# Two FFN and mixing layers in split fp32 on one core: earlier start of the next sublayer, another order of an attention pair, and a final update spread over three engines

## The chip, the cores and the metric

The kernel runs on one core of a Trainium2 chip. The metric is device time in microseconds (us) of one execution. The engines of the core are TensorE (PE; its weight loads are listed as PEld), VectorE (DVE), ScalarE (ACT), GpSimd (POOL) and SyncE (SP), whose queue issues the DMAs. Each engine works through its own instructions in the order in which the program emits them; semaphores hold an instruction until what it reads or overwrites is ready.

## The reference

Two layers work on 384 tokens of width 1024 in fp32: 128 prompt tokens and 256 latent tokens. Each layer has three sublayers: an FFN, a mixing sublayer and a second FFN. Cut to what matters here:

```
for l in range(2):
    h = modulate(x, npre[0], shift, scale)                  # rmsnorm * gain * (1 + scale) + shift
    x = x + 0.5 * gate * rmsnorm(swiglu(h, fw_in[0], fw_out[0]), npost[0])
    h = modulate(x, npre[1], ...)
    q, k, v, f, g = split(h @ w_in)                         # 512, 512, 512, 256, 512 columns
    o = concat(attn(q, k, v), fourier_mix(f), gmlp_mix(g))  # 8 heads of 64; rpb is a bias per head
    x = x + gate * rmsnorm(o @ w_out, npost[1])
    h = modulate(x, npre[2], ...)
    x = x + 0.5 * gate * rmsnorm(swiglu(h, fw_in[1], fw_out[1]), npost[2])
```

The attention of the latent tokens adds `rpb`, a table of biases for each head, to the scores, and also attends to 128 cached keys and values. The prompt tokens attend among themselves. The Fourier part transforms 256 channels, and the gated part passes 512 columns through gelu.

## The kernel before

Activations lie transposed, channels on partitions and tokens along the free axis, so that one tile is 128 channels by 384 tokens. Every weight product is done as three matmuls of a reduced fp32 type. A weight tile (`raw`, 128x1024) is split into `whi`, a cast on ACT (L160), and `wlo`, a subtraction on DVE (L170); `mm3` then multiplies hi by hi, hi by lo and lo by hi, eight times for a tile of eight k blocks. The weights of the whole program form one stream. Three raw tiles and six split tiles are held; the load of raw tile i+3 is put on SP's queue right after the subtraction that frees the buffer of raw tile i, and waits there for that subtraction. What the program puts on SP's queue later stands behind it. `take` hands the next split tile to the products and lets the stream split one tile more (`split_ahead`).

A sublayer ends in a `Post` object. `Post.add(m)` takes output tile m: a square on ACT (L483), its addition to `accy` on POOL (L485, for all but the first and the last tile), and a scaled copy `yg`. `all` sums the squares over partitions with matmuls against a matrix of ones (L206), `std` takes the root on ACT (L501). The next sublayer's `Enter` object is made by the function `after`, which computes the gain A on DVE (L227) and calls `begin`: five ACT instructions and three DVE instructions on tile 0 of x and of yg (L268 to L273). In an FFN `after` runs behind the products of output tile 6 of 0 to 7; in the mixing sublayer inside tile 7, behind its first two k blocks and behind the addition of tile 6. The next sublayer's `group` then runs its first five or six products before the norm of its input is known, carries two columns more per tile for the shift (386 columns), and multiplies by the reciprocal root afterwards (`biased`). From tile `switch` on, an FFN uses normed inputs (384 columns).

The mixing sublayer starts with `leave`: DVE scales a finished product tile into `t` (L460) and ACT applies gelu, or nothing for the Fourier and attention tiles, and writes it in two pieces (L716). Tiles 0 and 1 (`g0`, `g1`) and 2 and 3 (`ut`) are gelu tiles, tile 4 (`t0`) is a Fourier tile. `turn` transposes a tile on PE (L740) into one of two PSUM banks `px`; ACT copies it out (L787, L788 into `gv`). `channels` is the Fourier product over channels (L749) and uses a `px` bank too.

Attention goes in four pairs of heads. The order of a pair is a string, `PAIR` for the first three and `LAST` for the fourth. U is the value product of the pair before; A0 and A1 the scores; S0 and S1 the softmax steps on DVE and ACT (L830 adds the bias and takes the maximum, L833 and L839 are the exponentials, L842 to L845 the division), each for both heads of the pair (e0, e1); F00, F10, F01 and F11 the transposes of the probabilities (`flip`, L854 on PE, copied out by L858 and L860 on ACT), the first digit being the head; K0, K1, Q0, Q1, W0 and W1 are halves of the next pair's key, query and value products; L scales the next value tile, t transposes it (copied out by L914), k, c and q finish keys, cached keys and queries. The second half of K, Q and W also lets the stream split a tile. b issues the four DMAs of the next pair's `rpb` tables on SP (L683), and two additions on POOL for each head build `biases` from them (L689), which S0 of the next pair reads.

At the very end `finish` updates x for the last time: a reciprocal of the root on DVE (L509), then a multiplication (L514) and an addition (L515) for each pair of tiles, the 128 prompt tokens on POOL and the 256 latent tokens on DVE, and a DMA of each result (L516).

## Time and profile before

| | |
|---|---|
| median of 3 runs | 1476.79 us (1475.21 to 1476.86) |
| profiled execution, its own time | 1476.81 us |
| its span in the trace | 1475.0 us, so 1.8 us lie around the span |
| granted TensorE clock, mean | 0.991 |
| busy: PE, DVE, ACT, POOL | 98%, 78%, 47%, 14% |
| chain that ended last, by engine | PE 87%, DVE 5%, ACT 4% |

The busy shares say how much of the span an engine worked. The chain is followed back from the last instruction to what released each step. A PE at 98% leaves little idle time in all, so single places where PE waits are what the other views have to show: the list of PE's waits, and the timelines around them. In a timeline row the first number is the start in us from the beginning of the span, the second the time that the row covers, then engine, line, operation and tiles, the number of instructions that were drawn together, and in brackets the idle time before the row and what ended it.

### The profile page before, as it was taken

How to read it: one execution, taken by the hardware profiler on the slowest of the kernel's cores; microseconds unless marked ns; L12 is line 12 of the kernel's file. 1: busy time of each engine (PE TensorE's matmuls, PEld its weight loads, DVE VectorE, ACT ScalarE, POOL GpSimd, SP SyncE). 2: the span in 40 equal slices, each digit the busy share in tenths (PEclk: the TensorE clock that was granted, in tenths of full speed). 3: DMA queues.
4: the chain of work that ended last, by engine and by line, in shares of the span. 5: the costliest groups of instructions: out<-in, count | busy, mean ns of one | idle time of the engine just before them, and what ended most of it. 6: DMA issues, size and time to landing. Idle time of an engine off the chain costs nothing.

```text
span 1475.0 us, 22364 instructions
## 1 busy us (share of the span) xinstructions
PE 1443.1 (98%) x8459; PEld 1410.3 (96%) x8459; DVE 1151.2 (78%) x1859; ACT 688.3 (47%) x1262; POOL 207.7 (14%) x172
## 2 busy tenths in 40 slices
PE   9999999999999999999999999999999999999996
PEld 7999999999899999999999999999989999999995
DVE  3789999987768999969989998677877699755333
ACT  3663334346656753333257333433666657333330
POOL 1100000122214130001130300010323321100012
PEclk8999999999999999999999999999999999999998
DMA  9457777845533347757824577576254324554431
GB/s 377 157 175 238 242 243 240 262 151 148 130 83 100 120 152 248 240 175 252 260 83 158 190 241 220 166 220 199 85 144 110 122 63 152 173 172 134 118 104 43
DMA packets 87004, 254.04 MB, mean 172 GB/s; under 512 B 21872, under 2 KB 26224, under 8 KB 85872
## 3 DMA queue, kind: packets, MB, share of 16 engines
q1 hardware_dynamic: 86896, 252.62, 54.2%
q8 instruction: 66, 1.08, 0.3%
q14 instruction: 42, 0.34, 0.1%
HBM read 249.96 MB, written 2.62 MB: 171 GB/s over the span
## 4 chain that ended last, share of the span: by engine, by line
PE 87%; DVE 5%; ACT 4%; issue 2%; DMA 2%; SPq 0%; POOL 0%; DVEq 0%; ACTq 0%; POOLq 0%
PE ps L187 26%; PE ps L188 26%; PE ps L189 26%; DVE wlo L170 2%; ACT whi L160 1%; PE ps L416 1%; PE ps L417 1%; PE ps L419 1%; DMA x<-in_x_dram 1%; PE ps L206 1%; PE ps L870 1%; DMA raw<-in_ffn_w_in_dram 1%; PE ps L854 1%; PE ps L815 1%; DVE t L460 0%
## 5 line engine op out<-in xcount | busy, mean ns | idle before, releaser
L170 DVE TENSOR_TENSOR wlo<-raw,whi 128x1024 fp32r<-128x1024 f32 (+1 forms) x318 | 402.1, 1269 | 189.1 <-ACT whi L160 187.7
L160 ACT CAST whi<-raw 128x1024 fp32r<-128x1024 f32 x324 | 330.9, 1027 | 395.9 <-PE ps L188 364.1
L102 DVE CUSTOM_DVE_ANT_0 junk<-adaw,cb,adab 128x1024 bf16<-128x1024 f32 x256 | 334.5, 1307 | 11.2 <-DMA adaw<-in_ada_w_dram 6.6
L188 PE MATMUL ps<-nlo,whi 128*128 128x384 f32 x896 | 299.3, 334 | 0.0
L187 PE MATMUL ps<-nhi,whi 128*128 128x384 f32 x896 | 299.3, 334 | 0.0
L189 PE MATMUL ps<-nhi,wlo 128*128 128x384 f32 x896 | 299.3, 334 | 0.0
L187 PE MATMUL ps<-hhi,whi 128*128 128x386 f32 (+1 forms) x789 | 276.2, 350 | 0.0
L188 PE MATMUL ps<-hlo,whi 128*128 128x386 f32 (+1 forms) x789 | 269.0, 341 | 1.8 <-DVE hlo L244 1.7
L189 PE MATMUL ps<-hhi,wlo 128*128 128x386 f32 (+1 forms) x789 | 268.8, 341 | 0.7 <-DVE wlo L170 0.7
L187 PE MATMUL ps<-ahi,whi 128*128 128x384 f32 x768 | 257.2, 335 | 0.0
L188 PE MATMUL ps<-alo,whi 128*128 128x384 f32 x768 | 256.7, 334 | 0.0
L189 PE MATMUL ps<-ahi,wlo 128*128 128x384 f32 x768 | 256.6, 334 | 0.0
L485 POOL TENSOR_TENSOR accy<-accy,sqy 128x384 f32<-128x384 f32 x36 | 53.7, 1491 | 818.6 <-ACT sqy L483 818.4
L187 PEld LDWEIGHTS ps<-nhi,whi 128*128 128x128 f32 x896 | 168.2, 188 | 0.0
L188 PEld LDWEIGHTS ps<-nlo,whi 128*128 128x128 f32 x896 | 168.2, 188 | 0.0
L189 PEld LDWEIGHTS ps<-nhi,wlo 128*128 128x128 f32 x896 | 168.2, 188 | 0.0
L187 PEld LDWEIGHTS ps<-hhi,whi 128*128 128x128 f32 x789 | 149.9, 190 | 5.3 <-issue 3.1
L188 PEld LDWEIGHTS ps<-hlo,whi 128*128 128x128 f32 x789 | 149.9, 190 | 5.1 <-DVE hlo L244 3.6
L189 PEld LDWEIGHTS ps<-hhi,wlo 128*128 128x128 f32 x789 | 149.7, 190 | 1.3 <-DVE wlo L170 1.3
L187 PEld LDWEIGHTS ps<-ahi,whi 128*128 128x128 f32 x768 | 144.2, 188 | 0.3 <-DVE hlo L136 0.3
L188 PEld LDWEIGHTS ps<-alo,whi 128*128 128x128 f32 x768 | 144.2, 188 | 0.0
L189 PEld LDWEIGHTS ps<-ahi,wlo 128*128 128x128 f32 x768 | 144.2, 188 | 0.0
(177 smaller groups left out, 1412.6 us busy)
## 6 DMA issues: line engine op xcount, KB each, us to landing
raw<-in_ffn_w_in_dram SPq DMA_DIRECT2D x176, 512.0 KB, 4.1
adaw<-in_ada_w_dram SPq DMA_DIRECT2D x128, 512.0 KB, 4.2
raw<-in_ffn_w_out_dram SPq DMA_DIRECT2D x64, 512.0 KB, 4.2
raw<-in_w_in_dram SPq DMA_DIRECT2D x36, 512.0 KB, 4.3
raw<-in_ffn_w_out_dram SPq DMA_DIRECT2D x32, 384.0 KB, 3.7
piece<-in_ada_first_dram SPq DMA_DIRECT2D x8, 1024.0 KB, 9.2
raw<-in_w_out_dram SPq DMA_DIRECT2D x16, 512.0 KB, 3.6
rpb<-in_rpb_dram SPq DMA_DIRECT2D x32, 96.0 KB, 6.4
```

Source lines behind the costliest of these rows:

```text
L102: nc.vector.tensor_tensor_reduce(out=junk, in0=w, in1=cb[:, j, :], scale=1.0, scalar=adab[:, l, b, f:f + 1], op0=ALU.mult, op1=ALU.add, ac ...
L160: nc.scalar.copy(highs[i][:, :w], raws[i][:, :w])
L170: (eng or nc.vector).tensor_tensor(out=lo[:, :w], in0=raws[i][:, :w], in1=hi[:, :w], op=ALU.subtract)
L187: nc.tensor.matmul(ps, whi, hhi, start=start, stop=False)
L188: nc.tensor.matmul(ps, whi, hlo, start=False, stop=False)
L189: nc.tensor.matmul(ps, wlo, hhi, start=False, stop=stop)
L206: nc.tensor.matmul(ps, ones, sq, start=start, stop=stop)
L416: nc.tensor.matmul(ps[g][:, :n], w[g][0][:, ks], hhi, start=False, stop=False)
L417: nc.tensor.matmul(ps[g][:, :n], w[g][1][:, ks], hhi, start=False, stop=False)
L419: nc.tensor.matmul(ps[g][:, :n], w[g][0][:, ks], hlo, start=False, stop=False)
L485: nc.gpsimd.tensor_tensor(out=self.acc, in0=self.acc, in1=sq, op=ALU.add)
L815: nc.tensor.matmul(ps[e][:, :T], q[r, qs], k[r, :], start=i == 0, stop=i == 2)
```

## The change

Five places are changed.

1. In the FFN and in the mixing sublayer `after` runs ahead of the take and the products of output tile 6. In the mixing sublayer it so stands ahead of the splits of two weight tiles and of the additions of tiles 5 and 6 in each engine's order.
2. At the start of the mixing sublayer the Fourier tile `t0` leaves first, and the stream splits one tile between the `v` and the `ut` tiles.
3. In `PAIR` the flips of the first key tile stand behind the halves of the query product, and t, b and k behind Q1.
4. `switch` is rounded down where it was rounded up: FFNs with five first products use the normed input from tile 14 on in place of 16. The first FFN has six and is not touched.
5. `finish` is written anew: the sums of squares are taken with tokens on partitions, the root and reciprocal work on three columns, and matmuls spread the result over the partitions into a PSUM bank. DVE multiplies tile by tile; the addition is done on POOL (tiles 0, 2, 4, 6), on PE with a copy out by ACT (tiles 1, 3, 5) or on DVE (tile 7), and each tile has its DMA.

```diff
@@ -37,7 +37,7 @@
 GROUP = 5
 LEAD = 3
 FIRST = 6
-PAIR = "U A0 K0 S0 A1 K1 L F00 S1 Q0 F10 t b k Q1 c n F01 F11 q W0 d W1"
+PAIR = "U A0 K0 S0 A1 K1 L Q0 F00 S1 F10 Q1 t b k c n F01 F11 q W0 d W1"
 LOADS = "S1 w0 S0 x0 k0 w1 x3 w2 S2 x1 S3 x2 w3 S4 S5 S6 x4 S7 x5 w4 c1 c0 x6 w5 x7"
@@ -501,19 +501,43 @@
             nc.scalar.activation(self.sy, self.ps, AF.Sqrt, scale=1.0 / D, bias=eps[:, 0:1])
         def finish(self):
-            self.all()
-            self.std()
-
-            r, yg = self.sy, self.yg
-            for _, b, e in RANGES:
-                nc.vector.reciprocal(r[:, b:e], r[:, b:e])
-            for m in range(0, KT, 2):
-                for (_, b, e), eng in zip(RANGES, (nc.gpsimd, nc.vector)):
-                    new, old = yg[:, m:m + 2, b:e], x[:, m:m + 2, b:e]
-                    rb = r[:, b:e].unsqueeze(1).to_broadcast([P, 2, e - b])
-                    eng.tensor_tensor(out=new, in0=new, in1=rb, op=ALU.mult)
-                    eng.tensor_tensor(out=new, in0=new, in1=old, op=ALU.add)
-                    nc.sync.dma_start(out=o["y"][:, m:m + 2, b:e], in_=new)
+
+            yg, c = self.yg, 3
+            sums = [bank(px)[:, :2 * c].rearrange("p (t j) -> p t j", j=2) for _ in range(2)]
+            for ps, sq in zip(sums, (self.acc, self.sq)):
+                for t in range(c):
+                    nc.tensor.matmul(ps[:, t, :], sq[:, t * P:t * P + P], ones[:, :2], start=True, stop=True)
+                if sq is self.acc:
+                    early = small("sy")[:, :c]
+                    nc.scalar.activation(early, ps[:, :, 0], AF.Identity, scale=1.0 / D, bias=eps[:, 0:1])
+            held = {}
+
+            def hold(m):
+                held[m] = bank()[:, :T]
+                nc.tensor.matmul(held[m], ident, x[:, m, :], start=True, stop=False)
+
+            hold(1)
+            r = small("r")[:, :c]
+            nc.vector.scalar_tensor_tensor(out=r, in0=sums[1][:, :, 0], scalar=1.0 / D, in1=early, op0=ALU.mult, op1=ALU.add)
+            nc.scalar.activation(r, r, AF.Sqrt)
+            nc.vector.reciprocal(r, r)
+            out = act.tile([P, KT, T], F32, tag="nlo", name="out")
+            rb = bank()[:, :T]
+            for t in range(c):
+                nc.tensor.matmul(rb[:, t * P:t * P + P], r[:, t:t + 1].to_broadcast([P, P]), ident, start=True, stop=True)
+            hold(3)
+            for m in range(KT):
+                new = yg[:, m, :]
+                nc.vector.tensor_tensor(out=new, in0=new, in1=rb, op=ALU.mult)
+                if m == 1:
+                    hold(5)
+                if m in held:
+                    nc.tensor.matmul(held[m], ident, new, start=False, stop=True)
+                    new = out[:, m, :]
+                    nc.scalar.copy(new, held[m])
+                else:
+                    (nc.vector if m == KT - 1 else nc.gpsimd).tensor_tensor(out=new, in0=new, in1=x[:, m, :], op=ALU.add)
+                nc.sync.dma_start(out=o["y"][:, m, :], in_=new)
     def spread(n, i, of):
         return n * (i + 1) // of - n * i // of
@@ -525,7 +549,7 @@
             ahi = fp.tile([P, FT, T], F32R, name="ahi")
             alo = fp.tile([P, FT, T], F32R, name="alo")
-            switch = len(ps) + KT + 2 + len(ps) % 2
+            switch = len(ps) + KT + 2 - len(ps) % 2
             base = at[0]
             def leave(m):
@@ -628,6 +652,8 @@
             post = Post(l, s)
             last = None
             for m in range(KT):
+                if m == KT - 2:
+                    after(post)
                 p = bank()[:, :T]
                 for c, (b, e) in enumerate(((0, 8), (8, 16), (16, 22))):
                     w, = take()
@@ -637,8 +663,6 @@
                     if m < KT - 1:
                         ada_some(spread(ada_out, m * 3 + c, 3 * KT - 3))
                 last = p
-                if m == KT - 2:
-                    after(post)
             post.add(KT - 1, last)
         return post
@@ -776,13 +800,13 @@
+            t0 = leave(ps[4], v[:, 2, :T], SAME)
             g0 = leave(ps[0], v[:, 0, :T], GELU)
             g1 = leave(ps[1], v[:, 1, :T], GELU)
+            split_to(at[0] + 3)
             leave(ps[2], ut[:, 0, :], GELU)
             leave(ps[3], ut[:, 1, :], GELU)
-            pf0 = ps[4]
             split_to(at[0] + HOLD - 1)
-            t0 = leave(pf0, v[:, 2, :T], SAME)
             pf1 = project(False)
             nc.scalar.copy(gv[:, :, 0:P], turn(g0))
             nc.scalar.copy(gv[:, :, P:], turn(g1))
@@ -967,13 +991,13 @@
                 products(p, w3[i], oparts, [7])
             enter.restore()
             for m in range(3, KT):
+                if m == KT - 2:
+                    after(post, following)
                 w, = take()
                 p = bank()[:, :T]
                 products(p, w, oparts, range(2))
                 for i in range(3) if m == 3 else [m - 1]:
                     post.add(i, outs[i])
-                if m == KT - 1:
-                    after(post, following)
                 products(p, w, oparts, range(2, KT - 1))
                 products(p, w, oparts, [KT - 1])
                 outs.append(p)
```

Three places of the order that the changed program gives its engines follow; line numbers grow by 24 in this part of the file. First ACT at the start of layer 0's mixing sublayer, before, from the table load for gelu to t0's two pieces (v takes g0, g1 and t0, one after the other in pieces of 128 and 256 columns):

```order
L716 ACT_TABLE_LOAD
L716 ACTIVATE v<-t,b 128x128
L716 ACTIVATE v<-t,b 128x256
L716 ACTIVATE v<-t,b 128x128
L716 ACTIVATE v<-t,b 128x256
L716 ACTIVATE ut<-t,b 128x128
L716 ACTIVATE ut<-t,b 128x256
L716 ACTIVATE ut<-t,b 128x128
L716 ACTIVATE ut<-t,b 128x256
L160 CAST whi<-raw 128x1024 x3
L716 ACTIVATE v<-t,b 128x128
L716 ACTIVATE v<-t,b 128x256
```

and now:

```order
L740 ACTIVATE v<-t,b 128x128
L740 ACTIVATE v<-t,b 128x256
L740 ACT_TABLE_LOAD
L740 ACTIVATE v<-t,b 128x128
L740 ACTIVATE v<-t,b 128x256
L740 ACTIVATE v<-t,b 128x128
L740 ACTIVATE v<-t,b 128x256
L160 CAST whi<-raw 128x1024
L740 ACTIVATE ut<-t,b 128x128
L740 ACTIVATE ut<-t,b 128x256
L740 ACTIVATE ut<-t,b 128x128
L740 ACTIVATE ut<-t,b 128x256
```

The table load stands behind the two pieces of t0, and a cast stands between the gelu tiles; two casts and then the copies into gv follow the last row now, where the copies followed t0's pieces before. Next ACT in a pair of heads, before, from the copies of F00 (L858, L860) past the exponentials of S1 (L833), the copies of F10 and of the turned value tile (L914), the keys (L721, L722) and the cast that Q1 brings, to F01 and F11:

```order
L858 COPY pt<-ps 128x3x128
L860 COPY pt<-ps 128x128
L833 ACTIVATE p,st<-p,st 128x384 x2
L858 COPY pt<-ps 128x3x128
L860 COPY pt<-ps 128x128
L914 COPY v<-ps 128x3x128
L721 ACTIVATE kp<-t,b 128x128
L722 ACTIVATE qk<-t,b 128x256
L160 CAST whi<-raw 128x1024
L133 CAST qk<-ck 128x128
L858 COPY pt<-ps 128x3x128 x2
```

and now:

```order
L882 COPY pt<-ps 128x3x128
L884 COPY pt<-ps 128x128
L857 ACTIVATE p,st<-p,st 128x384 x2
L882 COPY pt<-ps 128x3x128
L884 COPY pt<-ps 128x128
L160 CAST whi<-raw 128x1024
L938 COPY v<-ps 128x3x128
L745 ACTIVATE kp<-t,b 128x128
L746 ACTIVATE qk<-t,b 128x256
L133 CAST qk<-ck 128x128
L882 COPY pt<-ps 128x3x128 x2
```

Q1's cast has moved ahead of the copy of the turned tile. Last SP's queue over the first two pairs, before, where in_w_in and in_w_out are weights of the stream and gw, gb are tables of the gated part:

```order
L153 DMA raw<-in_w_in_dram 128x1024 x3
L683 DMA rpb<-in_rpb_dram 64x6x64 x4
L153 DMA raw<-in_w_out_dram 128x1024
L944 DMA gw<-in_gmlp_w_dram 128x512
L946 DMA gb<-in_gmlp_b_dram 64x128 x4
L153 DMA raw<-in_w_out_dram 128x1024 x2
L683 DMA rpb<-in_rpb_dram 64x6x64 x4
L153 DMA raw<-in_w_out_dram 128x1024
L950 DMA scratch<-in_dft_s_dram 128x516
L951 DMA dft_p<-in_dft_p_dram 128x256
```

and now:

```order
L153 DMA raw<-in_w_in_dram 128x1024 x3
L153 DMA raw<-in_w_out_dram 128x1024
L707 DMA rpb<-in_rpb_dram 64x6x64 x4
L968 DMA gw<-in_gmlp_w_dram 128x512
L970 DMA gb<-in_gmlp_b_dram 64x128 x4
L153 DMA raw<-in_w_out_dram 128x1024 x3
L707 DMA rpb<-in_rpb_dram 64x6x64 x4
L974 DMA scratch<-in_dft_s_dram 128x516
L975 DMA dft_p<-in_dft_p_dram 128x256
```

The load that Q1's split brings, the last raw row ahead of each rpb row, stood behind the rpb tables and stands ahead of them now.

## Rows read from the trace of the kernel before

**Rows 1.** The page, part 1: busy time, share of the span and instructions of each engine.

```profile
PE 1443.1 (98%) x8459; PEld 1410.3 (96%) x8459; DVE 1151.2 (78%) x1859; ACT 688.3 (47%) x1262; POOL 207.7 (14%) x172
```

**Rows 2.** PE's waits over the whole span: engine, tile and line that waited, what it waited for; then us in total, times, longest.

```profile
PE ps L749 <- ACT gv L787: 4.4, 2, 2.2
PE ps L740 <- ACT pt L860: 2.7, 3, 1.3
PE ps L206 <- ACT sqy L483: 2.4, 3, 1.1
PE ps L206 <- POOL accy L485: 1.3, 1, 1.3
```

**Rows 3.** Timelines of ACT and of DVE at the start of layer 0's mixing sublayer (337 to 352 us), and the first softmax row of head e1 of its first pair.

```profile
338.27 1.28 ACT L716 ACT_TABLE_LOAD   x1
340.53 1.50 ACT L716 ACTIVATE v<-t,b 128x128 f32<-128x128 f32 x4 [0.97 <-DVE t L460]
343.31 2.94 ACT L160 CAST whi<-raw 128x1024 fp32r<-128x1024 f32 x3
349.15 0.46 ACT L787 COPY gv<-ps 128x384 f32<-128x384 f32 x1
349.88 0.81 ACT L716 ACTIVATE t<-t,b 128x128 f32<-128x128 f32 x2
...
337.35 2.55 DVE L426 RECIPROCAL r<-r 128x384 f32<-128x384 f32 x1 [0.59 <-ACT r L290]
339.93 0.56 DVE L460 TENSOR_TENSOR t<-ps,r 128x384 f32<-128x384 f32 x1
365.53 0.56 DVE L830 CUSTOM_DVE_ANT_0 p<-ps,biases 128x384 f32<-128x384 f32 x1 [0.21 <-POOL biases L689]
```

**Rows 4.** Timelines of DVE, of ACT and of PE over the third pair of layer 0 and the start of the fourth (402 to 425 us). The L830 rows are S0's for head e1, L170 at 405.75 is the split that K1 brings and at 413.06 the one that Q1 brings, L845 ends S0 of the fourth pair, and the PE row is the flip F10 of the fourth pair.

```profile
402.74 0.55 DVE L830 CUSTOM_DVE_ANT_0 p<-ps,biases 128x384 f32<-128x384 f32 x1
405.75 1.22 DVE L170 TENSOR_TENSOR wlo<-raw,whi 128x1024 fp32r<-128x1024 f32 x1
413.06 1.23 DVE L170 TENSOR_TENSOR wlo<-raw,whi 128x1024 fp32r<-128x1024 f32 x1 [0.45 <-ACT whi L160]
421.07 0.55 DVE L830 CUSTOM_DVE_ANT_0 p<-ps,biases 128x384 f32<-128x384 f32 x1
423.90 0.28 DVE L845 TENSOR_SCALAR p<-p,st 128x128 f32<-128x128 f32 x1
...
407.54 0.80 ACT L716 ACTIVATE t<-t,b 128x128 f32<-128x128 f32 x2 [1.82 <-DVE t L460]
408.25 0.46 ACT L858 COPY pt<-ps 128x384 f32<-128x384 f32 x1
409.97 0.47 ACT L858 COPY pt<-ps 128x384 f32<-128x384 f32 x1
410.49 0.50 ACT L914 COPY v<-ps 128x384 f32<-128x384 f32 x1
412.00 1.03 ACT L160 CAST whi<-raw 128x1024 fp32r<-128x1024 f32 x1
...
424.86 0.60 PE L854 MATMUL ps<-ident,p 128*128 128x128 f32 x4
```

**Rows 5.** Timelines of SP's queue and of POOL in the second and third pair of layer 0: the issues of the next pair's rpb tables, and the additions that wait for them.

```profile
389.78 2.66 SPq L683 DMA_DIRECT2D rpb<-in_rpb_dram  x4
407.76 3.58 SPq L683 DMA_DIRECT2D rpb<-in_rpb_dram  x4
...
396.77 1.42 POOL L689 TENSOR_TENSOR biases<-rpb,cmask 128x256 f32<-128x256 f32 x2 [13.84 <-DMA rpb<-in_rpb_dram]
399.01 1.57 POOL L689 TENSOR_TENSOR biases<-rpb,cmask 128x256 f32<-128x256 f32 x2 [0.81 <-DMA rpb<-in_rpb_dram]
414.50 3.72 POOL L689 TENSOR_TENSOR biases<-rpb,cmask 128x256 f32<-128x256 f32 x4 [10.41 <-DMA rpb<-in_rpb_dram]
```

**Rows 6.** Timelines of ACT and POOL at the end of layer 0's mixing sublayer (460 to 466 us).

```profile
462.65 0.40 ACT L268 ACTIVATE accx<-x,A 128x128 f32<-128x128 f32 x1 [1.20 <-DVE A L227]
464.12 0.48 ACT L483 ACTIVATE sqy<-ps 128x384 f32<-128x384 f32 x1
...
460.97 1.61 POOL L485 TENSOR_TENSOR accy<-accy,sqy 128x384 f32<-128x384 f32 x1 [0.34 <-ACT sqy L483]
```

**Rows 7.** Timelines of ACT and PE at the end of the first FFN (306 to 313 us).

```profile
309.29 0.48 ACT L483 ACTIVATE sqy<-ps 128x384 f32<-128x384 f32 x1
...
311.55 0.91 PE L206 MATMUL ps<-accy,ones 128*128 128x384 f32 x2 [1.31 <-POOL accy L485]
```

**Rows 8.** Groups of PE's instructions by line, tile and shape over the whole span: instructions, busy us, mean ns of one, idle time before.

```profile
L188 PE MATMUL ps<-nlo,whi 128*128 128x384 f32 x896 | 299.3, 334 | 0.0
L188 PE MATMUL ps<-hlo,whi 128*128 128x386 f32 x725 | 247.4, 341 | 1.8 <-DVE hlo L244 1.7
```

**Rows 9.** Timelines of ACT and DVE at the end of the program (1460 to 1472 us).

```profile
1460.44 0.58 ACT L501 ACTIVATE sy<-ps,eps 128x384 f32<-128x384 f32 x1 [1.00 <-PE ps L206]
...
1461.12 2.56 DVE L509 RECIPROCAL sy<-sy 128x128 f32<-128x128 f32 x2 [0.91 <-ACT sy L501]
1463.72 1.19 DVE L514 TENSOR_TENSOR yg<-yg,sy 128x512 f32<-128x512 f32 x1
1471.19 0.69 DVE L515 TENSOR_TENSOR yg<-yg,x 128x512 f32<-128x512 f32 x1
```

## Prediction

> **What bounds the kernel now.** I read first the busy times: PE works 98% of the span [rows 1]. So nothing that only frees DVE, ACT or POOL can pay; the change can win where PE waits, at the very end where PE is done, or by fewer columns, and it can lose wherever it makes PE wait. The second view is the list of PE's waits [rows 2]. All four of its rows lie at places that the change touches: the start of the mixing sublayers (L749, 4.4 us in two waits), the turned tile of a pair (L740, 2.7 us in three) and the ends of sublayers (L206, 2.4 and 1.3 us). Together they hold 10.8 us, and that is about what the edits in the loops could win at most. The third view is the timeline around each such place, on the engines that PE waits for; there the reader is to see what stands in front of the awaited instruction in its own engine's order. The time that is not PE's is the tail: from the end of the last root (1460.44 + 0.58) to the end of the span at 1475.0, 14.0 us pass [rows 9].
>
> **The start of the mixing sublayer.** Today the gelu table load runs at 338.27 to 339.55, while DVE computes the reciprocal (337.35 to 339.90) for which everything waits, and the first piece leaves on ACT at 340.53 [rows 3]. The load costs nothing: that reciprocal is its cover. In the new order the load stands behind t0's two pieces, so ACT does t0 at 340.53 to 341.33, loads until 342.61, and gelu for g0 and g1 (half of 1.50 us for four pieces each, so 1.5 us) ends at 344.1 in place of 342.0. Then a cast (1.0) ends at 345.1, its subtraction on DVE (1.2) at 346.3, and only behind that DVE scales the ut tiles (0.55 each) to 347.4, which ACT finishes at 348.3. Two casts end at 350.2, so gv's copy starts at about 350.2 and not at 349.15, and the turned Fourier tile of the second leave, behind two more subtractions on DVE (to 351.7), leaves at 352.3 and not at 349.88. The chain on ACT and DVE is so 2.4 us later. That this chain and not PE bounds the stretch I take from two waits: PE waits 2.2 us for gv in each layer [rows 2], and e1's first softmax row waits for POOL, whose tables are issued behind the same splits [rows 3]. I carry +2.4 us per layer into the first softmax: its row for head e1, 365.53 [rows 3], becomes 367.95. If PE's cover further on absorbs the delay, it is 1.0 (the gv copy alone).
>
> ACT goes from the cast's end at 338.26 straight into the 1.28 us of the load [rows 3]; nothing is drained there. The Trainium skill (ScalarE: Activation LUTs, What ACT_TABLE_LOAD costs) gives 1283 ns for the load and 1380 ns for a drain with each switch. The first figure is this trace's; by the second the load that is now in the open would cost 1.4 us more in each layer, and the sum would be 2.8 us higher than mine.
>
> **The pair.** The new order gives the softmax of S0 the time of Q0 as cover, and the flips go as one block; the waits of L740 (2.7 us) for F00's copies should go, since 12 more products stand between. But Q1's split comes ahead of the turned tile's copy on ACT, and its load ahead of rpb on SP. The first price: F11 waits for the copy, which now stands behind the cast (1.03); the cast cannot begin until Q1's last product has read the buffer. After 0.5 us of transposes PE then lacks some 0.6 us, and a pair that PE paces takes 18.9 us where e1's rows now show 421.07 - 402.74 = 18.3 [rows 4].
>
> The second price is a loop through SP. Now rpb is issued behind K1's subtraction, which ends 405.75 + 1.22 = 406.97, 4.2 us after S0's e1 row; the issue is at 407.76 [rows 4, 5]. In the new order it stands behind Q1's load and so behind Q1's subtraction. From e1 that subtraction is, by the rows of the same instructions [rows 4]: to the value tile on ACT 407.54 - 402.74 = 4.80; its two pieces 0.71; F00's copies 0.51; S1's exponentials 1.21 (the 1.72 from 408.25 to 409.97 less 0.51); F10's copies 0.52; cast to subtraction 1.06; subtraction 1.23: 10.05 us. To the rpb issue 0.45. From the issue to POOL's first addition for e0 I read 396.77 - 389.78 = 7.0, for e1 399.01 - 389.78 = 9.2, and for e1 of the next pair, third of four additions (414.50 + 1.9), at most 8.7 [rows 5]; I take 8.9. One addition, 0.75. So next S0's e1 comes no earlier than 10.05 + 0.45 + 8.9 + 0.75 = 20.15 us after this one, with 8.7 and 9.2 as landing 19.95 and 20.45; PE's pace is 18.3 to 18.9. Today that bias is ready at 414.50 + 2.8 = 417.3 at the latest and needed at 421.07, 3.8 us of slack; the loop takes 10.05 + 0.45 - 5.0 = 5.5 to 5.8 us of it.
> From 367.95 three periods lead to 428.4 for the fourth pair's e1, where the row of before is 421.07: 7.3 us later. There F10 needs the end of the division, now 424.18, and begins at 424.86 [rows 4], so 0.7 of it is slack and **+6.6 us per layer** remain, the start's 2.4 included and the won waits of L740 used up. With the landing at 8.7 it is 6.0, at 9.2 7.5. Two layers: **+13.2**, from 12 to 15.
>
> **`after` in the mixing sublayer.** The wait is 1.1 us in each layer, for the square of tile 7 (464.12), which today stands behind `begin`'s five instructions (462.65 to 464.2) [rows 2, 6]. Moving these forward takes them out of that place, but here ACT runs behind PE, since casts wait for raw loads; the same work must be done ahead of tile 7's square, and what now stands directly ahead of it is tile 6's square, whose addition on POOL takes 1.61 [rows 6]. POOL then ends at about 465.0, after PE asks. I take **+0.7** per layer; the bounds are -1.1 (the wait goes) and +0.9. Both: +1.4.
>
> **`after` in the FFNs.** Only the first one waits, 1.3 us at 311.55 for POOL's addition of tile 6, whose square on ACT came at 309.29, behind `begin` [rows 7]. With `begin` two products earlier the square is freed, but `after`'s gain A still stands behind the modulation's sums on DVE, and the next group is bound by DVE. I take **-1.1**, bounds -0.5 and -1.9. The FFNs without a wait gain nothing.
>
> **`switch`.** Two tiles in each of three FFNs, 24 matmuls each, go from 386 to 384 columns: 144 matmuls. By the mean durations, 341 and 334 ns [rows 8], 1.0 us; since matmuls overlap, by the columns' share of the pitch 0.4. I take **-0.5**. The normed tiles are ready by then.
>
> **The end.** Today root 0.58, reciprocal 2.56, then eight DVE steps of 0.68 to 1.2 (slow while POOL works beside them) from 1463.72 to 1471.88, and 3.1 us for the last DMA [rows 9]. New: small operations on three columns and two rounds of short matmuls until about 1461.7 (an estimate: two waits of 0.9 between engines, as in the brackets there, shorter operations between). Eight multiplications from a PSUM bank at 0.5 (that of [rows 3] is 0.56 alone, with a pitch of about 0.5) end at 1465.6, and tile 7's addition at about 1466.2. POOL's four additions from 1462.2: at 1.0 each they end with tile 6 at 1466.5, at 1.6 [rows 6] at 1468.6; I take 1.25, so 1467.2, plus 3.1 is 1470.3: **-4.7** against 1475.0, bounds -3.3 and -5.8.
>
> **The sum.** +13.2 + 1.4 - 1.1 - 0.5 - 4.7 = +8.3 us on the profiled execution's 1476.81 us (the median is 1476.79): **1485.1 us**. Its own bounds, the terms' ends taken together and not all at one end, are 1481.5 and 1489.
>
> **The rivals.** *The biases come in time.* If e1's tables land 7.0 us after issue, as e0's do [rows 5], the loop is 18.2 us and PE paces the pairs. Then the mixing sublayers lose 2.4 at the start and 0.6 in three pairs, less 2.7/2 and what cover there is: about +2.8 each. 5.6 + 1.4 - 1.1 - 0.5 - 4.7 = +0.7: 1477.5 us. For it: the first two tables are there early. Against it: in both pairs read, e1's came later.
> *The other side, faster: PE's slack swallows both delays.* Q0 ahead of F00 puts 2.1 us of products between S0 and the flip that needs it. If the delays at the start and at each S0 stay under that cover and the cast hides behind the transposes, the mixing sublayers come out even, and only the ends count: 0 - 1.1 - 0.5 - 4.7 = -6.3, 1470.5 us. It decides at an S0 delay of about 2.8 us (2.1 and the 0.7 of slack); by the loop e1's row is 5.5 us late in the third pair (408.25 against 402.74) and 7.3 in the fourth, which has no Q0 to cover it.
> *The change does all that it says.* All of L749's, L740's and L206's waits go (-10.8) and the tail gives 4.7, with -0.5: 1461 us. Against it stands that gv's copy is later, not earlier.
> *Longer landings.* If the loads ahead on the queue delay rpb by 1.5 us more, three periods in two layers are 9 us longer less slack: 1490 to 1496 us.
>
> **How the numbers follow.** Forecast 0.48 (1481.5 to 1489), biases in time 0.17, even mixing 0.17, all gained 0.10, longer landings 0.08. The range leaves out the last two: 1468 to 1489.5. About 0.2% (3 us) is what a measurement of this kernel can tell from no change. Slower by more: 0.48 + 0.08 + 0.05 of the second case; within: 0.12 of it; faster: 0.27.
>
> **What would show it.** Right: POOL's L689 rows directly ahead of S0's e1 row, e1 rows 20 us apart, PE waits at the flips of pairs three and four for DVE; wrong: e1 rows 18 to 19 us apart. The load at 341.3 on ACT, with gv's copy 1 us later, shows the start. L206 waiting for POOL in the mixing sublayers shows the fourth step, no L206 wait for the first FFN the fifth, a last DMA issued at about 1467 the tail. The forecast falls if rpb lands within 7 us, or if PE's waits at the flips are short of 2 us in all.

## The result: slower by 1.2%

The changed kernel takes 1493.6 us (median of 4 runs, 1490.7 to 1495.94) beside 1476.76 us before: a ratio of 1.0116, 95% interval 1.0093 to 1.0139. The profiled execution took 1495.5 us, with a span of 1493.7 us. The direction was forecast, and the size was not: 17 us in place of 8.3, above the range's end of 1489.5.

The list of PE's waits, which before named gv, the turned tile and the sums of squares [rows 2], now reads:

```profile
PE ps L878 <- ACT pt L884: 5.3, 5, 1.2
PE ps L206 <- POOL accy L485: 4.6, 2, 2.3
PE ps L878 <- ACT v L938: 4.6, 6, 0.8
PE ps L773 <- ACT gv L811: 3.6, 2, 1.8
PE ps L878 <- DVE p L867: 2.2, 4, 0.8
PE ps L764 <- ACT pt L884: 1.7, 4, 0.7
```

L878 is the flip, L764 the turned tile, L773 the channels. The wait for the turned tile has shrunk (2.7 to 1.7 us), but the flips, which had waited once for 0.9 us before, wait 12 us in all.

Where the time went shows best by stretches between rows of PE that both kernels have. A stretch runs from the start of one such row to the next; values in us, layer 0 / layer 1, from the timelines of PE:

| stretch | before | changed |
|---|---|---|
| norm's sum (L206, accx) to A0 of the first pair | 25.91 / 24.32 | 26.93 / 26.94 |
| A0 of the first to A0 of the fourth pair | 57.49 / 59.06 | 67.74 / 63.95 |
| A0 of the fourth pair to the sum of accy | 43.89 / 43.72 | 46.34 / 48.84 |
| that sum to the next norm's sum | 24.77 / 24.60 | 24.73 / 23.40 |
| start to the norm's sum after the first FFN | 335.35 | 333.37 |
| three later FFNs, norm's sum to accy's sum | 257.57, 257.56, 257.56 | 257.37, 257.38, 257.38 |
| last sum of accy to the end of the span | 16.32 | 12.39 |

The mixing sublayers lose 13.7 and 11.4 us, 15.1 of the 25.1 in the first three pairs. The stretch with the first FFN is 2.0 shorter, `switch` gives 0.6 and the end 3.9.

The loop that was forecast stands in the timelines of DVE (S0's row for head e1 in the four pairs of layer 0, and the subtraction of the first pair's Q1), of SP and of POOL:

```profile
367.44 0.56 DVE L854 CUSTOM_DVE_ANT_0 p<-ps,biases 128x384 f32<-128x384 f32 x1 [1.66 <-POOL biases L713]
376.01 1.23 DVE L170 TENSOR_TENSOR wlo<-raw,whi 128x1024 fp32r<-128x1024 f32 x1 [0.86 <-ACT whi L160]
387.83 0.56 DVE L854 CUSTOM_DVE_ANT_0 p<-ps,biases 128x384 f32<-128x384 f32 x1 [1.48 <-POOL biases L713]
411.16 0.56 DVE L854 CUSTOM_DVE_ANT_0 p<-ps,biases 128x384 f32<-128x384 f32 x1 [3.87 <-POOL biases L713]
431.63 0.56 DVE L854 CUSTOM_DVE_ANT_0 p<-ps,biases 128x384 f32<-128x384 f32 x1 [1.19 <-POOL biases L713]
...
377.68 2.62 SPq L707 DMA_DIRECT2D rpb<-in_rpb_dram  x4
398.46 2.66 SPq L707 DMA_DIRECT2D rpb<-in_rpb_dram  x4
421.40 2.65 SPq L707 DMA_DIRECT2D rpb<-in_rpb_dram  x4
...
387.06 1.42 POOL L713 TENSOR_TENSOR biases<-rpb,cmask 128x256 f32<-128x256 f32 x2 [0.84 <-DMA rpb<-in_rpb_dram]
410.40 1.43 POOL L713 TENSOR_TENSOR biases<-rpb,cmask 128x256 f32<-128x256 f32 x2 [3.22 <-DMA rpb<-in_rpb_dram]
430.87 1.41 POOL L713 TENSOR_TENSOR biases<-rpb,cmask 128x256 f32<-128x256 f32 x2 [1.03 <-DMA rpb<-in_rpb_dram]
```

Each e1 row waits for POOL, where those of [rows 4] did not. From e1 at 367.44 Q1's subtraction ends at 377.24, 9.8 later; rpb goes out at 377.68; POOL begins e1's bias at 387.06, 9.4 after that; the next e1 is 0.8 later. The periods are 20.4, 23.3 and 20.5 us.

At the start the load now stands in the open, as ACT's timeline shows:

```profile
338.55 0.80 ACT L740 ACTIVATE v<-t,b 128x128 f32<-128x128 f32 x2 [2.27 <-DVE t L460]
339.37 1.28 ACT L740 ACT_TABLE_LOAD   x1
340.66 1.49 ACT L740 ACTIVATE v<-t,b 128x128 f32<-128x128 f32 x4
...
348.20 0.47 ACT L811 COPY gv<-ps 128x384 f32<-128x384 f32 x1
...
350.37 0.80 ACT L740 ACTIVATE t<-t,b 128x128 f32<-128x128 f32 x2 [1.33 <-DVE t L460]
```

Counted from the norm's sum (333.37 here, 335.35 before), gv's copy is 1.0 us later than in [rows 3] and the second leave 2.5. ACT goes from t0's last piece (end 339.35) into the load and from the load (end 340.65) into gelu, so no drain is seen beside the 1.28 us here either; the Trainium skill (ScalarE: Activation LUTs, What ACT_TABLE_LOAD costs) puts 1.38 us more on each switch, which this trace does not bear out.

At the end of the mixing sublayer the sum waits for POOL; timelines of POOL and PE:

```profile
472.72 1.60 POOL L485 TENSOR_TENSOR accy<-accy,sqy 128x384 f32<-128x384 f32 x1 [0.34 <-ACT sqy L483]
...
474.38 0.91 PE L206 MATMUL ps<-accy,ones 128*128 128x384 f32 x2 [2.31 <-POOL accy L485]
475.12 0.84 PE L206 MATMUL ps<-sqy,ones 128*128 128x384 f32 x2
```

And the end, in DVE, POOL and SP:

```profile
1484.72 3.80 DVE L531 TENSOR_TENSOR yg<-yg,ps 128x384 f32<-128x384 f32 x8 [1.03 <-PE ps L527]
...
1485.36 3.87 POOL L539 TENSOR_TENSOR yg<-yg,x 128x384 f32<-128x384 f32 x4 [13.56 <-DVE yg L531]
...
1489.65 0.90 SPq L540 DMA_DIRECT2D out_dram<-yg  x2
```

The eight multiplications take 0.48 each and POOL's additions 0.97, but the last two DMAs are issued one after the other from 1489.65, 4.1 us ahead of the end of the span; before, 3.1 us lay between DVE's last step and the end.

One thing was not in the forecast: PE's clock. Windows of the changed kernel: stretch, length, busy us and instructions of PE, PEld, DVE, ACT and POOL, PE's granted clock, DMA share, GB/s:

```profile
372.00:375.00 3.00, 1.24 (x7) 0.69 (x6) 1.81 (x8) 3.00 (x11) 0.00 (x0) 1.00 0.49 175
375.00:378.00 3.00, 2.14 (x10) 1.91 (x11) 1.91 (x4) 1.55 (x4) 0.00 (x0) 0.80 0.00 0
378.00:381.00 3.00, 3.00 (x13) 3.00 (x13) 2.30 (x5) 1.54 (x5) 0.00 (x0) 0.63 0.78 198
474.00:477.00 3.00, 2.62 (x8) 2.10 (x9) 0.67 (x2) 0.58 (x1) 0.32 (x1) 0.80 0.59 194
477.00:480.00 3.00, 3.00 (x13) 3.00 (x13) 2.21 (x5) 0.00 (x0) 0.00 (x0) 0.64 0.02 5
```

Behind the waits in a pair and at the end of a mixing sublayer the granted clock is at its lower level (0.50, 1.2 GHz) for part of these windows: (1 - 0.80) x 3 + (1 - 0.63) x 3 = 1.7 us of full-speed work lost in the first two, 1.7 in the last two. In the mixing sublayers of the profiled execution of before this happens once, in that of the changed kernel six times. The number is not fixed for a kernel: over its four executions the changed kernel's mean granted clock lies between 0.989 and 0.996.

### The profile page after: what moved, and what is told of

Its sections match the earlier page's. It is cut to its first block, busy times and chain, and to the rows that moved or that the text cites. A ratio compares the mean times of both kernels' runs of the same rounds, so it can differ in the third digit from the quotient of the medians.

```text
span 1493.7 us, 22376 instructions
## 1 busy us (share of the span) xinstructions
PE 1459.6 (98%) x8485; PEld 1420.3 (95%) x8485; DVE 1140.2 (76%) x1845; ACT 689.3 (46%) x1263; POOL 199.6 (13%) x168
## 4 chain that ended last, share of the span: by engine, by line
PE 82%; DVE 5%; ACT 5%; DMA 4%; issue 2%; SPq 1%; POOL 1%; ACTq 0%; DVEq 0%; POOLq 0%
PE ps L187 25%; PE ps L189 25%; PE ps L188 25%; DMA rpb<-in_rpb_dram 3%; DVE wlo L170 2%; ACT whi L160 2%; PE ps L416 1%; PE ps L417 1%; PE ps L419 1%; PE ps L206 1%; SPq L707 1%; ACT p L857 1%; PE ps L335 1%; PE ps L357 1%; DVE t L460 1%
## 5 line engine op out<-in xcount | busy, mean ns | idle before, releaser
L170 DVE TENSOR_TENSOR wlo<-raw,whi 128x1024 fp32r<-128x1024 f32 (+1 forms) x318 | 398.9, 1259 | 199.4 <-ACT whi L160 198.4
L188 PE MATMUL ps<-nlo,whi 128*128 128x384 f32 x944 | 315.3, 334 | 0.0
L187 PE MATMUL ps<-nhi,whi 128*128 128x384 f32 x944 | 315.3, 334 | 0.0
L189 PE MATMUL ps<-nhi,wlo 128*128 128x384 f32 x944 | 315.3, 334 | 0.0
L187 PE MATMUL ps<-hhi,whi 128*128 128x386 f32 (+1 forms) x741 | 262.9, 355 | 0.0
L188 PE MATMUL ps<-hlo,whi 128*128 128x386 f32 (+1 forms) x741 | 256.2, 346 | 1.8 <-DVE hlo L244 1.7
L189 PE MATMUL ps<-hhi,wlo 128*128 128x386 f32 (+1 forms) x741 | 255.6, 345 | 0.7 <-DVE wlo L170 0.7
L187 PEld LDWEIGHTS ps<-nhi,whi 128*128 128x128 f32 x944 | 177.2, 188 | 0.0
L188 PEld LDWEIGHTS ps<-nlo,whi 128*128 128x128 f32 x944 | 177.2, 188 | 0.0
L189 PEld LDWEIGHTS ps<-nhi,wlo 128*128 128x128 f32 x944 | 177.2, 188 | 0.0
L187 PEld LDWEIGHTS ps<-hhi,whi 128*128 128x128 f32 x741 | 143.3, 193 | 5.2 <-issue 3.1
```

Of the source, the lines that this page charges most:

```text
L170: (eng or nc.vector).tensor_tensor(out=lo[:, :w], in0=raws[i][:, :w], in1=hi[:, :w], op=ALU.subtract)
L187: nc.tensor.matmul(ps, whi, hhi, start=start, stop=False)
L188: nc.tensor.matmul(ps, whi, hlo, start=False, stop=False)
L189: nc.tensor.matmul(ps, wlo, hhi, start=False, stop=stop)
```

## The experiments

Every kernel was timed beside the kernel before, on the same chip. The ratios compare these; the medians of before differ by 1.7 us between the sets.

| run | median, us | before beside it | ratio, 95% interval |
|---|---|---|---|
| e1_pair_old | 1476.68 | 1474.23 | 1.0019 (1.0005 to 1.0033) |
| e2_mix_after_old | 1491.76 | 1474.23 | 1.0111 (1.0093 to 1.0129) |
| e3_start_old | 1488.97 | 1474.23 | 1.0094 (1.0077 to 1.0111) |
| e4_three_undone | 1470.0 | 1474.23 | 0.9963 (0.9949 to 0.9977) |
| e5_b_early | 1480.57 | 1475.48 | 1.0041 (1.0026 to 1.0056) |
| e6_fill5 | 1495.49 | 1475.48 | 1.0135 (1.0118 to 1.0151) |
| e7_best_w0 | 1476.66 | 1475.48 | 1.0008 (0.9997 to 1.0019) |
| e8_best_w0_rpb0 | 1482.71 | 1475.48 | 1.0047 (1.0030 to 1.0065) |
| e9_old_b_late | 1497.94 | 1475.6 | 1.0153 (1.0139 to 1.0167) |
| e10_best_fill3 | 1469.09 | 1475.6 | 0.9956 (0.9942 to 0.9969) |
| e11_best_rpb1 | 1468.7 | 1475.6 | 0.9953 (0.9941 to 0.9966) |
| e12_best_both | 1469.26 | 1473.93 | 0.9965 (0.9953 to 0.9978) |
| e13_pair_fill4 | 1494.47 | 1473.93 | 1.0139 (1.0122 to 1.0157) |

**The parts, one undone at a time.**

```diff
-PAIR = "U A0 K0 S0 A1 K1 L Q0 F00 S1 F10 Q1 t b k c n F01 F11 q W0 d W1"
+PAIR = "U A0 K0 S0 A1 K1 L F00 S1 Q0 F10 t b k Q1 c n F01 F11 q W0 d W1"
```

> The changed kernel with the old order of a pair, all else as changed. Theory (the rpb loop through SP's queue sets the pairs, and each cluster of waits on PE is followed by some 3.4 us at half clock): from A0 of the first pair to A0 of the fourth 57 to 59 us in each layer in place of 67.7 and 64.0, no POOL wait at S0 after the first pair, the clock falls only at the start and the end of a mixing sublayer; about 17 us less than 1493.6, so 1473 to 1479 us. Rival (the later start of the mixing sublayer is what is carried through the pairs, whatever their order): 1485 us or more.

The three pairs take 58.2 and 61.0 us. By the ratios (1.0116 - 1.0019) the new pair costs 14 us, by the stretches of both mixing sublayers 16.4 (165.7 + 163.1 against 156.0 + 156.5). The rival falls. One fall of the clock was seen in a first pair too, which the expectation did not have. In the two strings, what moves is F00, now behind Q0 beside F10, and t, b and k, now behind Q1.

e2 puts `after` back behind tile 6's addition:

> The changed kernel with the old place of after in the mixing sublayer alone. Theory: PE's wait for accy on POOL (2.3 us in each layer) goes, the wait for the last square (1.1) returns, and the fall of the clock behind the end of layer 0's mixing sublayer (1.7 us) goes: 1488 to 1491.5 us. Rival (the place is neutral, since ACT has the same work): 1492.5 to 1494.5 us.

A0 of the fourth pair to the sum takes 44.3 / 44.2 in place of 46.3 / 48.8, and the fall of the clock behind layer 0's end goes; the mixing sublayers are 2.8 and 1.7 us shorter. The ratio falls by 0.0005 only, inside both intervals, and 1491.76 us lies between the two ranges: the timing does not tell the place from a neutral one, and the stretches of one execution speak for the theory.

e3 lets t0 leave last again:

> The changed kernel with the old order at the start of the mixing sublayer alone (table load under the reciprocal again). Theory: 1.0 and 2.6 us come back between the norm and A0 of the first pair, and the loop of the pairs starts that much earlier: 1488 to 1491 us. Rival (the start's delay is the cause of most of the 17 us): below 1482 us.

The start takes 24.35 / 25.91, 2.6 and 1.0 less, and the rival falls. The expectation had the two numbers in the other layers. In all kernels here but e8 the old order takes 24.3 us where the clock does not fall in it and 25.9 where it does, the new one 25.9 and 26.9. So the order costs 1.0 to 1.6 us in a layer, and the rest is a fall of the clock, which came in both layers of the changed kernel, in layer 0 of before and in layer 1 of e3.

e4 undoes all three and keeps `after` in the FFNs, `switch` and the new end:

> The changed kernel with the old pair, the old start and the old place of after in the mixing sublayer; what is left of the change is after in the FFNs, switch and the new end. Theory: the end of the first FFN 2.0, switch 0.2 in each of three FFNs, the end 4.0 us: 1469 to 1472 us. Rival (what an end wins is lost again behind it): 1474 to 1477 us.

It is faster than before by 0.37%. What the ends win stays won. Between e1 and e4 lie only the start and the place of `after` in the mixing sublayer: 1.0019 and 0.9963, or 8 us, clear of both intervals (7.6 us by the stretches of both mixing sublayers). So these two parts lose time together, although neither e2 nor e3 alone shows it beyond its interval.

**The loop.** e5 moves one token of the new pair:

```diff
-PAIR = "U A0 K0 S0 A1 K1 L Q0 F00 S1 F10 Q1 t b k c n F01 F11 q W0 d W1"
+PAIR = "U A0 K0 S0 b A1 K1 L Q0 F00 S1 F10 Q1 t k c n F01 F11 q W0 d W1"
```

> The changed kernel with one token of its pair moved: b, the rpb loads, stands right behind S0, so ahead of the loads that K1 and Q1 bring on SP; Q1's cast still stands ahead of the turned tile's copy. Theory (the rpb loop through SP sets the pairs): S0 of the second to fourth pair waits for POOL no longer, PE paces a pair at 18.9 us (F11 still waits 0.8 us for the copy behind the cast), A0 to A0 over three pairs 56.5 to 59 us in each layer in place of 67.7 and 64.0, no fall of the clock in the second and third pair: some 15 us less than the changed kernel. Rival (the cast ahead of the copy and the crowded two banks of the flips set the pairs): 62 us or more, at most 5 us less than the changed kernel.

S0's e1 rows of the second and third pair, from DVE's timeline, wait for nothing:

```profile
382.62 0.55 DVE L854 CUSTOM_DVE_ANT_0 p<-ps,biases 128x384 f32<-128x384 f32 x1
402.20 0.55 DVE L854 CUSTOM_DVE_ANT_0 p<-ps,biases 128x384 f32<-128x384 f32 x1
```

Both pairs take 19.17 us in both layers, 0.86 above the 18.31 of before; 0.62 of it is PE's wait at F11 for the copy behind the cast, forecast as 0.6, and the other 0.24 was not traced. The first pair takes 24.5 / 24.2: S0 waits 2.2 / 0.9 us there for tables that are loaded at the start and not by b, PE waits 3.6 / 3.1 us at the turned tile and the flips, and the clock falls once. So the pairs sum to 62.8 / 62.6, past the 59 of the theory and into the rival's range, but the time does not follow the rival: by the ratios (1.0116 - 1.0041) the kernel wins 11 us, where the rival had at most 5 and the theory 15.

e9 makes the reverse test, from e4: the old pair, with b alone behind Q1. PE, DVE, ACT and POOL have e4's order, instruction by instruction; on SP the rpb loads come one load later.

```diff
-PAIR = "U A0 K0 S0 A1 K1 L F00 S1 Q0 F10 t b k Q1 c n F01 F11 q W0 d W1"
+PAIR = "U A0 K0 S0 A1 K1 L F00 S1 Q0 F10 t k Q1 b c n F01 F11 q W0 d W1"
```

> e4_three_undone with one token of the old pair moved: b, the rpb loads, behind Q1, as the change has it; all other engines keep the old order, only SP's differs. Theory (the place of the rpb loads on SP is what the new pair loses by): the loads go out when Q1's subtraction is done, some 11 us after S0's row for e1, so with 9.4 to 10.6 us to POOL a pair takes 20.5 to 23 us, S0 waits for POOL in the second to fourth pair, and the clock falls at least once more in each layer: 10 to 20 us more than e4_three_undone, so 1480 to 1490 us. Rival (the flips and the cast on ACT and PE are what costs, SP's place is hidden): within 3 us of e4_three_undone.

It costs 28 us over e4, more than was expected: pairs of 20.9, 22.6 and 23.0 us in layer 0 (e4: 22.5, 19.1, 18.3), and 6.6 us more behind the fourth pair's A0 in each layer. The first head waits as well as the second:

```profile
382.00 0.56 DVE L853 CUSTOM_DVE_ANT_0 p<-ps,biases 128x384 f32<-128x384 f32 x1 [1.99 <-POOL biases L713]
384.23 0.56 DVE L853 CUSTOM_DVE_ANT_0 p<-ps,biases 128x384 f32<-128x384 f32 x1 [1.44 <-POOL biases L713]
```

So the place of the rpb loads on SP is shown as a cause in both directions, and e5 gives its share: 11 of the 14 us that the new pair costs. The other 3, which the intervals of e5 and e1 leave open, fall to the rest of the new order.

**The clock.** e6 gives PE work in its wait at the end:

```diff
         def __init__(self, l, s):
+            self.s = s
...
             self.ps = bank(px)[:, :T]
+            for _ in range(5 if self.s == 1 else 0):
+                sumsq(self.ps, self.yg[:, 0, :], True, True)
             sumsq(self.ps, self.acc, True, False)
```

> The changed kernel with five more matmuls of 384 columns ahead of the sum of squares at the end of each mixing sublayer, into the bank that the sum then overwrites, so that PE works during its wait for POOL; their results are not used. Theory (the fall to half clock follows PE's idle time, and costs 1.7 us each time): behind layer 0's mixing sublayer the granted clock stays at 1.00, and the stretch from the sum of squares to the next one is 1.5 us shorter (23.2 in place of 24.7); in layer 1, where the clock did not fall, no difference. Rival (the clock falls for what comes behind the wait, not for the idle time): 24.7 us and a granted clock below 0.7 as before.

The windows at the same place:

```profile
474.00:477.00 3.00, 3.00 (x15) 2.34 (x14) 0.64 (x2) 0.58 (x1) 0.00 (x0) 1.00 0.39 150
477.00:480.00 3.00, 3.00 (x19) 3.00 (x18) 2.93 (x8) 0.99 (x3) 0.00 (x0) 1.00 0.00 0
```

The clock stays at 1.00 and the stretch behind the sum is 23.29 us in place of 24.73, 1.4 less, as expected. That prices the fall. It does not show that the fillers kept the clock up: behind the same wait in layer 1 (2.27 us) the clock stayed up in the changed kernel too, without fillers, and the stretch is 23.40. Over its four executions e6 has a granted clock of 0.991 to 0.994, no better than the changed kernel's. The kernel gains nothing; the five matmuls (3.2 us) outlast the wait by 0.75 us.

e13 does the same inside the pairs:

> The changed kernel with four matmuls of 384 columns, whose results are not used, in each of the first three pairs at the places where PE waits behind Q1 (one ahead of the turned tile, two behind it, one ahead of F11; 0.65 us each). One reading (the falls of the clock in the pairs come on top of the loop): no fall in the pairs, and the three pairs of the two layers together, 131.7 us in the changed kernel, are 4 to 5 us shorter. The other (the loop through SP sets the pairs, and a slow PE is hidden in its waits): the falls go and the pairs stay within 2 us, so the whole of the pairs' loss is the loop's.

```profile
375.00:378.00 3.00, 2.87 (x17) 2.25 (x17) 1.79 (x4) 1.55 (x4) 0.00 (x0) 1.00 0.00 0
```

No fall is left in the pairs, and the granted clock of the five executions is 0.995 to 0.999, beside 0.989 to 0.996 in the changed kernel. The three pairs of the two layers take 132.0 us together where the changed kernel takes 131.7, and S0's e1 rows wait for POOL as before. So the second reading holds: the loop sets the pairs, and in its waits the slow clock is hidden.

**Toward a better kernel.** e7 combines e4 with the flips behind Q0, b behind S0 and W0 ahead of F01:

```diff
-PAIR = "U A0 K0 S0 A1 K1 L F00 S1 Q0 F10 t b k Q1 c n F01 F11 q W0 d W1"
+PAIR = "U A0 K0 S0 b A1 K1 L Q0 F00 S1 F10 Q1 t k c q n W0 F01 F11 d W1"
```

> The kernel with the three edits undone (e4_three_undone), and another order of a pair: the flips behind Q0 as in the change, b right behind S0, and W0 ahead of F01 and F11, so that these wait neither for the cast nor for the two banks. Theory: no wait of PE in the second and third pair, 18.0 to 18.4 us each, and 1 to 3 us less than e4_three_undone in all; the first pair still waits for its late tables. Rival (Q0 ahead of the flips costs as much as it covers): the same time as e4_three_undone within 1 us.

It is 4.5 thousandths, or 6.6 us, slower than e4, which neither reading had. The second and third pair take 19.5 to 19.9 us: now the value product of the next pair waits 0.7 to 1.1 us for the last flip's copy. The cover was only moved on, and the old order's 18.31 has none of these waits.

e8 changes the place of the first pair's tables in e7:

> e7_best_w0 with the first pair's rpb loads put on SP ahead of the first tile that leaves, not behind the splits. Theory (the first S0 waits for its tables): the POOL wait at S0 of the first pair goes, and with it up to 2.5 us of PE's wait at the first flips in each layer: 1 to 4 us less than e7_best_w0. Rival (the loads put first delay the weights behind them by as much): the same within 1 us or slower.

The first S0 waits for POOL no longer, but the rival holds: PE waits up to 3.1 us at the first A0 for the queries, whose weights come later, and the clock falls there; the start takes 29.1 / 27.0 us.

e10 to e12 start from e4. The edit of e10 and that of e11:

```diff
             pk = project(False)
+            idle = bank()[:, :T]
+            for _ in range(3):
+                sumsq(idle, v[:, 0, :T], True, True)
             channels(0, t0)
...
-            split_ahead()
             bias = [bias_of(0), bias_of(1)]
+            split_ahead()
```

> e4_three_undone with three matmuls of 384 columns, whose results are not used, in PE's wait for gv at the start of each mixing sublayer (2.2 us). Theory (idle PE time brings the half clock): the fall behind this wait, seen in layer 1 of e4_three_undone, goes, 1.7 us there; in layer 0, where the clock fell later, at the first flips, it may still fall there: 0 to 3.5 us less than e4_three_undone. Rival (the fillers push later work back): 1 us more or worse.

> e4_three_undone with the first pair's rpb loads ahead of one weight load on SP in place of behind it. Theory (the first S0 waits for tables): its POOL wait of 1.9 us in layer 0 shrinks by 1 us or more and the clock no longer falls in the first pair: 1 to 3 us less than e4_three_undone. Rival (as e8_best_w0_rpb0 showed for loads put first, the weight behind is late by as much): no gain, or up to 3 us more.

> e4_three_undone with both of the edits of e10_best_fill3 and e11_best_rpb1: three matmuls in PE's wait for gv, and the first rpb loads ahead of one weight load. Theory (each took away the falls of the clock by another way): no fall of the clock left in either, so little over the better of the two, 0 to 1.5 us less: 1467 to 1469 us. Rival (their gains add up): 1464 to 1466 us.

In e11 the first S0's row for e1 no longer waits for POOL (1.87 us in e4). The profiled executions of all three show no fall of the clock in the mixing sublayers, and their three pairs take 58 to 59 us. They lie 0.35 to 0.47% below the kernel before, and cannot be told from each other or surely from e4; the gains do not add up. The fillers' part is not shown: e11 has none, its PE still waits 2.2 us for gv, and its clock stays up there as well; other executions of e11 have a mean granted clock down to 0.994.

## Why the prediction was right in kind and wrong in size

1. **The failed step is the landing in the loop's sum "10.05 + 0.45 + 8.9 + 0.75".** The loop itself is there as forecast, and its first two terms measured 10.2 to 10.6 us together over six periods (forecast 10.5). The landing, from the rpb issue to POOL's addition for e1, was taken as 8.9 us, between the 9.2 of [rows 5] and an "at most 8.7". It measured 9.4, 11.9 and 9.5 in layer 0 (rows above) and 9.8, 10.6 and 10.5 in layer 1: 10.3 on average, 1.4 us more in each of six periods, 8.3 us in all. Together with the first tables of layer 0 (point 3) this brings the fourth pair's e1 row 12.5 and 11.4 us later than before, where 7.3 was forecast.

As a reading the 8.9 was nearly right: over the six such loads of the kernel before, the landing is 8.6 to 10.0 us, 9.1 on average. What failed was to carry it over to another place on SP's queue. The rival "Longer landings", 1490 to 1496 us, had the size right with 1.5 us more, and got a chance of 0.08; that size belonged in the range. Its reason, the loads ahead on the queue, is not what differs: in both kernels a weight load goes out 0.4 to 0.8 us ahead of rpb. What differs is what follows. SP's queue before (the rpb issues are those of 389.78 in [rows 5]) and now (those of 398.46 above):

```profile
389.35 0.33 SPq L153 DMA_DIRECT2D raw<-in_w_out_dram  x1
396.67 0.33 SPq L153 DMA_DIRECT2D raw<-in_w_out_dram  x1
...
398.04 0.33 SPq L153 DMA_DIRECT2D raw<-in_w_out_dram  x1
401.21 0.71 SPq L974 DMA_DIRECT2D scratch<-in_dft_s_dram  x1
404.56 1.01 SPq L153 DMA_DIRECT2D raw<-in_w_out_dram  x1
```

Before, the next load follows 6.6 to 7.0 us behind the first rpb issue, now 2.7 to 6.1. The other kernels agree: those with the old pair unchanged (e1, e4, e10 to e12) have the next load at 6.6 to 7.0 us and landings of 8.9 to 9.0 on average, those with the loads elsewhere (e2, e3, e5 to e9, e13) have it at 2.7 to 6.4 and landings of 10.1 to 10.8. That the later loads slow the tables down is thus likely; no run moved those loads alone, so it is not shown.

2. **F11 behind the cast:** 0.6 us was forecast; the wait is 0.62 and the pair 0.86 longer (e5), so this term held. The slack that Q0 should give in the rival "the other side" (2.8 us) did not save the pairs.
3. **The start:** gv is 1.0 and the second leave 2.5 us later by the trace, forecast 1.0 and 2.4. The first e1 row came 34.1 and 32.7 us behind the norm's sum, forecast 32.6. The 1.5 us too many in layer 0 are again a landing: the first tables took 12.9 us to POOL's addition there, 11.5 in layer 1 and in both layers of before.
4. **`after` in the mixing sublayer:** PE waits 2.3 us for POOL, as the step had it. From the last product to the next group's first, layer 0 takes 3.75 us (471.73 to 475.48), 0.9 more than before (462.30 to 465.11), forecast 0.7. What was left out is the clock behind it: the stretch is 24.73 us with a fall in layer 0, 23.40 without one in layer 1.
5. **The first FFN's end:** from one and the same product of PE, 1500 matmuls ahead of the sum, to the next norm's sum 1.8 us are gained (287.55 to 285.74), forecast 1.1 with 1.9 as its bound; the wait for POOL is gone. The other 0.2 of the 2.0 lies further ahead, where nothing was changed. **`switch`:** 0.6, forecast 0.5.
6. **The end:** 3.9 us were gained, forecast 4.7. POOL's additions took 0.97 and not 1.25; but DVE begins 3.4 us after the first sum (forecast 3.0), and the last two DMAs go out one behind the other.

The accounts: mixing sublayers up to the sum of accy, without its wait, +21.8 (forecast 13.2); that wait and the stretch behind it +3.3 (1.4); the stretch with the first FFN -2.0; `switch` -0.6; the end -3.9; together +18.6, where the spans differ by 18.7. The median's difference is 16.8. Profiled executions differ by some 4 us ahead of the first FFN's end already (its sum stands at 305.8 to 310.0 in kernels that are the same up to there): from 18 to 30 us the granted clock is 0.57 in the changed kernel and 1.00 in e1.

## What to carry to other kernels

When a reordering moves a wait past an issue, follow everything that stands behind that wait on the issuing queue: one token of the order, on SP alone, cost 28 us here (e9) while the other engines' order stayed the same. If what is delayed returns to the place that delays it, write the loop as a sum and compare its period with the pace of the busiest engine; the term with the widest rows, here the landing of a transfer, then sets the range, once per round. A landing read at one place of a queue need not hold at another: it was 9.1 us before the move and 10.3 behind it. Test a change of many parts with each part undone, and with all suspects undone together: the pair lost 14 us by its own run, two more parts lost 8 only seen together, and the rest made a faster kernel.

## What was not expected of the hardware

The same wait does not always bring the clock down. Before, PE's wait of 2.2 us for gv is followed by the lower level in layer 0 and not in layer 1, and in e11 in neither layer. Executions of one kernel differ in it too: those of before have a mean granted clock of 0.990 to 0.996, so a single trace does not tell whether an edit kept the clock up. Where it falls, it costs 1.7 us of full-speed work. Unused matmuls in the waits of the pairs went with a higher granted clock over all executions (e13), those in one wait at the end did not (e6). And a slow clock costs nothing where PE would have waited anyway: three falls in the pairs, some 5 us of lost work, were not in the time (e13).
